# A sum over graph edges: 8 or 4 of 32 destination blocks by row gathers, and with or without a cast in the gather

## The chip, the cores and the metric

The kernel runs on one core of one Trainium2 chip. The metric is the device time of one execution in microseconds (us). TensorE does the matmuls, VectorE the comparisons and elementwise work, ScalarE copies and casts out of PSUM, GpSimd (POOL in the profile) issues the row gathers, and SyncE (SP) issues the plain loads and stores. The engines run on their own and wait for each other by semaphores; each takes its instructions in the order in which the program was written.

## The reference

There are 4096 nodes with 128 float32 features and 65536 edges. Each edge adds the feature row of its source node to the output row of its destination node:

```python
num_nodes, num_edges, dim = 4096, 65536, 128
output = np.zeros((num_nodes, dim), dtype=np.float32)
for i in range(len(edge_index_src)):
    output[edge_index_dst[i]] += node_features[edge_index_src[i]]
```

## The kernel before

The output is made in 32 destination blocks of 128 rows. The feature rows are kept in two parts, a rounded one and the rest, side by side as 256 values (`xr` in SBUF, `x3d` in DRAM, 1 KB a row), so that matmuls in the reduced float32 format add up to the full value; the two halves of a result are added at the end.

**Pass 1** (before the loop) holds the edges as 24 chunks of 22 columns by 128 partitions, worked on in six quads of four chunks. It ranks the edges of each chunk by destination block and moves them with matmuls against permutation matrices, so that in `sa` and `sbk` every chunk has, for every destination block, a column of up to 128 edges, one in each partition: `sbk` holds the source block, `sa` a code of the source and destination rows within their blocks.

**Gathered blocks.** The first `KG` = 8 destination blocks (L27) are summed from gathered rows. For a block `d` and a quad `q`, `gather` (L320 to L327) issues four indirect DMAs on POOL; each fetches 128 rows of `x3d` by the indices in `gidx` into a quarter of a tile `rows`, which is declared float32r, while `x3d` is float32. There are six such tiles (`GB`, pool `xg`). `gather_key` compares the destination rows with a counter on VectorE (`ohg`) and casts the result on ScalarE (`ohgf`, L333). `gather_sum` (L341) does four matmuls of 256 columns into `psg`; after six quads the block is evacuated (L348). The 48 tiles stand in a fixed `order`. `add_up(n)` sums up to the n-th, and before each sum it issues gathers up to `GB` tiles ahead (`issue`, L361), of which the last has to wait until the tile before the current one is summed and its buffer free.

**Dense blocks.** The other 24 blocks are made by matmuls alone. For each block, `pass2` sorts the edges once more by their 32 source blocks. It works on a group of blocks together (`GROUPS`, L28: 4, 4, 8 and 8), in steps: for a group of four, bucket comparisons with column sums (L551, L560), payloads (L495), counts and ranks (L574, L577, L512); for a group of eight, bucket comparisons with sums (L480, L488), payloads, running counts (L503), masking and ranks (L507, L512); then, for each pair of blocks, permutations on VectorE (L212, tile `p`), matmuls (L533), a ScalarE copy `pa` (L536) and the keys of the pair on VectorE (L543). With the keys, `onehots` (L591) builds two one-hot matrices of 128 by 4096 on VectorE (tile `oh`). `blocks(k)` (L601) multiplies them for four source blocks into `psa`, one of two PSUM buffers, giving the counts of each source row in each destination row, and ScalarE casts these into `a` (L603). `product(k)` (L607) multiplies `a` with `xr`, 256 columns at a time, into `pso`.

**The loop** (L662 to L687) has one slot for each dense block, 24 in all. In each slot VectorE first makes what is pending of keys, then the key one-hots (`prepare`), the one-hots of the next slot's block, and the first part of the steps that the table `STEPS` (L30 to L32) names for this slot as (group, number of steps). TensorE does the slot's 32 block matmuls, in four turns with the 32 products of the previous slot's block, then the matmuls of the steps, then `add_up(n)`, where n spreads the tiles that are left evenly over the slots. Group 0 and two steps of group 1 are done before the loop, and nine tiles are summed there. ScalarE's queue holds the casts of the key one-hots ahead of the slot's casts of `a`. Order and steps are written out by hand; there is no planner.

Of the kernel before, what the change touches and what calls it, by code (L numbers as in the profile page):

```python
# [9 lines left out]
F32 = mybir.dt.float32  # L10
# [13 lines left out]
CODE0 = 0x2000  # L24
ROW0 = P + (CODE0 >> 7)
BIG = 4096.0
KG = 8  # L27
GROUPS = (4, 4, 8, 8)  # L28

STEPS = {0: [(1, 1)], 1: [(1, 1)], 2: [(1, 1), (2, 1)], 3: [(2, 1)], 4: [(2, 1)], 5: [(2, 1)],  # L30
         6: [(2, 1)], 7: [(2, 1)], 9: [(2, 1), (3, 1)], 11: [(2, 1)], 12: [(3, 2)], 13: [(3, 1)],
         14: [(3, 1)], 16: [(3, 1)], 18: [(3, 1)], 20: [(3, 1)]}  # L32


WIN = ((0, 7, 0, 64), (7, 14, 4, 100), (14, NJ, 20, P))
# [49 lines left out]
def _fast(ctx, tc, X, src32, dst32, out, ident, fmax, flag_i, x3d, T):  # L85
# [66 lines left out]
    for r in (slice(0, P), slice(P, ROW0)):  # L152
        for i in range(2):
            nc.sync.dma_start(
                out=x3d[r, i * P:(i + 1) * P].rearrange("p (j m) -> p j m", j=4),
                in_=zrow[:r.stop - r.start, i])
# [122 lines left out]
    def place(q):  # L279

        at = (q % 2 * QH + q // 2) * 4
        return slice(at, at + 4)
# [21 lines left out]

    gidx = sb1.tile([P, NCH, KG], I32, name="gidx")
    gkey = sb1.tile([P, NCH, KG, 2], U16, name="gkey")
    gslo = sb1.tile([P, NCH, KG], U16, name="gslo")

    def gather_keys(q):
        cs = place(q)  # L310
        code = sa[:, cs, :KG].bitcast(U16)
        V.tensor_single_scalar(out=gslo[:, cs, :], in_=code, scalar=7, op=OP.logical_shift_right)
        V.tensor_single_scalar(out=gkey[:, cs, :, :], scalar=127, op=OP.bitwise_and,
                               in_=code[:, :, :, None].to_broadcast([P, 4, KG, 2]))
        V.scalar_tensor_tensor(out=gidx[:, cs, :], in0=sbk[:, cs, :KG], scalar=float(P),
                               in1=gslo[:, cs, :], op0=OP.mult, op1=OP.add)
# [3 lines left out]
    def gather(d, q):  # L320
        t = xg.tile([P, 4, 2 * P], F32R, name="rows", tag="xg")
        for l in range(4):
            G.indirect_dma_start(  # L323
                out=t[:, l, :], out_offset=None, in_=x3d[:, :],
                in_offset=bass.IndirectOffsetOnAxis(ap=gidx[:, place(q).start + l, d:d + 1],
                                                    axis=0))
        rows[d, q] = t  # L327
# [33 lines left out]
    def issue(n):  # L361
        nonlocal issued
        while issued < min(n, ready):
            gather(*order[issued])
            issued += 1
# [81 lines left out]
    for t in p2b:  # L447
        for h in range(2):
            S.copy(out=t[:, h * NH:(h + 1) * NH, (1 - h) * 64:(2 - h) * 64],
                   in_=zero.to_broadcast([P, NH, 64]))  # L450
    first = [KG + sum(GROUPS[:g]) for g in range(len(GROUPS))]
    keys2 = {}

    def pass2(g):

        d0, gd = first[g], GROUPS[g]
        kk = 4 if gd % 4 == 0 else 2
# [153 lines left out]
    def flag():  # L611

        ng = len(GROUPS)
        full = sb1.tile([P, NCH * NB], BF16, name="full", tag="o0")
# [11 lines left out]

    todo = [pass2(g) for g in range(len(GROUPS))]

    def run(fs):
        for f in fs:  # L630
            f()
# [27 lines left out]
    n0 = summed  # L659
    flat_slots = [(g, i) for g, gd in enumerate(GROUPS) for i in range(gd)]  # L660
    slots = len(flat_slots)
    for slot, (g, i) in enumerate(flat_slots):  # L662
        n = n0 + (len(order) - n0) * (slot + 1) // slots
        run(pending)
        steps = [todo[pg].pop(0) for pg, k in STEPS.get(slot, ()) for _ in range(k)]
        pending = [f for st in steps for f in st[2:]]
# [115 lines left out]
```

## Time and profile before

| | |
|---|---|
| time, median of 3 runs | 442.68 us (440.57 to 444.94) |
| the profiled execution | 445.17 us, span 443.4 us |
| mean granted TensorE clock | 0.815 of full |
| busy in the span | TensorE 306.0 us, VectorE 263.1, POOL 217.9, ScalarE 191.0 |
| indirect DMAs | 192, 25.18 MB |

The span runs from the first to the last instruction; the execution is a little longer. A busy TensorE is one with a matmul in flight, not one at its peak. The time before the first `psa` matmul, 140.4 us, is pass 1 and the first steps of pass 2; the rest is the loop and the last block's products.

### The profile page before, as it was taken

The page shows a single profiled execution, that of the slowest core. Times are in us where ns is not written, and L with a number is a line of the kernel's source. Part 1 is how long each engine was busy: PE and PEld are TensorE (multiplying, and loading weights), DVE is VectorE, ACT ScalarE, POOL GpSimd, SP SyncE. Part 2 cuts the span into 40 slices and gives each one's busy share as a digit, 9 for nine tenths or more (in the row PEclk, how much of TensorE's full clock was granted, in tenths as well). Part 3 has the DMA queues.
Part 4 walks back from the last instruction along what each step waited for, and adds up shares of the span by engine and source line. Part 5 has one row for each costly group of instructions (what it writes and reads, how often), then busy time and mean ns, then how long its engine had stood idle before and what let it go on. Part 6 is the DMA issues. An engine that isn't in the chain of part 4 may idle for free.

```text
span 443.4 us, 8588 instructions
## 1 busy us (share of the span) xinstructions
PE 306.0 (69%) x3580; PEld 278.1 (63%) x3584; DVE 263.1 (59%) x438; ACT 191.0 (43%) x381; POOL 217.9 (49%) x222
## 2 busy tenths in 40 slices
PE   0887646736606688795966868487888668686896
PEld 0677435725605378694965858487787657575886
DVE  5999825927209516797826548158985428282740
ACT  3764213206103544372454344355355426363572
POOL 6534747156563334574836444636773544545300
PEclk9999658665655578897989759979799889798899
DMA  9833423043341222233333222422432333424200
GB/s 254 239 129 90 103 65 85 14 94 70 69 99 38 59 49 49 65 79 78 86 76 89 66 61 44 106 55 52 108 86 54 79 88 73 89 55 102 61 14 19
DMA packets 42504, 35.37 MB, mean 80 GB/s; under 512 B 5344, under 2 KB 42208, under 8 KB 42464
## 3 DMA queue, kind: packets, MB, share of 16 engines
q0 software_dynamic: 27648, 25.18, 25.9%
q1 hardware_dynamic: 14672, 9.11, 7.2%
q8 instruction: 28, 0.46, 0.4%
q10 hardware_dynamic: 144, 0.52, 0.3%
q14 instruction: 12, 0.10, 0.1%
HBM read 28.31 MB, written 6.49 MB: 78 GB/s over the span
## 4 chain that ended last, share of the span: by engine, by line
PE 45%; DVE 14%; issue 14%; ACT 12%; another core or an unknown queue 12%; DMA 1%; ACTq 0%; DVEq 0%
PE pso L607 18%; PE psa L601 10%; ACT a L603 6%; PE psg L341 5%; DVE oh L212 4%; PE ps L533 4%; DVE v L273 3%; ACT ohgf L333 3%; DVE p L212 3%; PE psm L297 2%; PE psr L512 2%; ACT cum L252 1%; PE psb L488 1%; PE psc L577 1%
## 5 line engine op out<-in xcount | busy, mean ns | idle before, releaser
L323 POOL DMA_INDIRECT rows<-x3d,gidx x192 | 200.8, 1046 | 184.6 <-PE psg L341 110.3
L603 ACT CAST a<-psa 128x512 fp32r<-128x512 f32 x192 | 104.6, 589 | 102.2 <-remote 63.6
L607 PE MATMUL pso<-xr,a 128*128 128x256 f32 x768 | 125.9, 312 | 0.0
L601 PE MATMUL psa<-oh 128*128 128x128 bf16 x768 | 71.7, 235 | 66.9 <-issue 40.8
L607 PEld LDWEIGHTS pso<-xr,a 128*128 128x128 f32 x768 | 108.6, 210 | 0.0
L601 PEld LDWEIGHTS <-oh 128*128 128x128 bf16 x768 | 52.5, 105 | 78.4 <-issue 73.3
L212 DVE TENSOR_TENSOR oh<-psi,slo 128x4096 bf16<-128x4096 uint16 x24 | 54.9, 2286 | 33.6 <-PE psa L601 30.9
L212 DVE TENSOR_TENSOR p<-psi,rank 128x768 bf16<-128x768 uint16 (+4 forms) x120 | 52.9, 509 | 12.4 <-ACT rank L517 8.9
L212 DVE TENSOR_TENSOR oh<-psi,dlo 128x4096 bf16<-128x4096 uint16 x24 | 54.8, 2282 | 0.0
L543 DVE TENSOR_SCALAR slo<-pa 128x128 uint16<-128x128 uint16 x12 | 2.7, 226 | 83.9 <-ACT pa L536 83.9
L341 PE MATMUL psg<-rows,ohgf 128*128 128x256 f32 x192 | 38.4, 354 | 4.5 <-ACT ohgf L333 4.5
L341 PEld LDWEIGHTS psg<-rows,ohgf 128*128 128x128 f32 x192 | 33.8, 256 | 5.1 <-ACT ohgf L333 5.0
L297 PE MATMUL psm<-v,p 128*128 128x64 bf16 x512 | 25.3, 208 | 16.7 <-issue 14.8
L252 ACT ACTIVATE cum<-psc,minus 128x512 bf16<-128x512 f32 (+1 forms) x36 | 21.9, 649 | 29.1 <-remote 12.7
L333 ACT CAST ohgf<-ohg 128x512 fp32r<-128x512 bf16 x48 | 27.9, 624 | 13.5 <-DVE ohg L212 13.5
L297 PEld LDWEIGHTS <-p 128*128 128x128 bf16 x512 | 21.8, 107 | 19.0 <-issue 16.6
L533 PEld LDWEIGHTS <-p 128*128 128x128 bf16 x576 | 19.3, 107 | 16.4 <-DVE p L212 15.6
L212 DVE TENSOR_TENSOR ohg<-psi,gkey 128x512 bf16<-128x512 uint16 x48 | 18.3, 417 | 0.0
L197 POOL TENSOR_TENSOR xr<-xf,xr 128x512 fp32r<-128x512 f32 x8 | 11.8, 1495 | 13.3 <-ACT xr L193 13.3
L249 PEld LDWEIGHTS <-sums 128*128 128x128 bf16 x126 | 11.4, 109 | 9.8 <-issue 6.6
L533 PE MATMUL ps<-v,p 128*128 128x32 bf16 x480 | 17.0, 195 | 0.0
L245 PE MATMUL psc<-oh,early 128*128 128x512 bf16 (+1 forms) x33 | 13.6, 412 | 3.3 <-ACT cum L252 2.7
(83 smaller groups left out, 252.1 us busy)
## 6 DMA issues: line engine op xcount, KB each, us to landing
x3d<-xr SPq DMA_DIRECT2D x4, 1024.0 KB
rows<-x3d,gidx POOLq DMA_INDIRECT x192
xf<-in_node_features_dram SPq DMA_DIRECT2D x4, 512.0 KB
out_dram<-res SPq DMA_DIRECT2D x32, 64.0 KB
raw<-in_edge_index_src_dram ACTq DMA_DIRECT2D x1, 512.0 KB
raw<-in_edge_index_dst_dram SPq DMA_DIRECT2D x1, 512.0 KB
x3d<-p SPq DMA_DIRECT2D x2, 64.0 KB
x3d<-p SPq DMA_DIRECT2D x2, 32.0 KB
```

Source lines behind the costliest of these rows:

```text
L212: V.tensor_tensor(out=dst.rearrange("p i (m k) -> p i m k", k=2), in0=io.rearrange("p i (m k) -> p i m k", k=2), in1=keys2[:, :, None, :]. ...
L245: PE.matmul(out=psc[:, :n * P], lhsT=early[:], rhs=oh1q(q)[:, 4 * j0:4 * (j0 + n), :].rearrange("p t b -> p (t b)"), start=True, stop=j0 + ...
L252: S.activation(out=cum[:, :, 4 * j0:4 * (j0 + n)], func=RELU, bias=minus[:], in_=psc[:, :n * P].rearrange("p (t b) -> p b t", b=NB))
L273: V.tensor_tensor(out=v1[q][:, :, k, :].rearrange("p t (b k) -> p t b k", k=2), in0=oh1q(q).rearrange("p t (b k) -> p t b k", k=2), in1=ke ...
L297: PE.matmul(out=psm[:, l * 64:(l + 1) * 64], lhsT=t[:, l % 2, j, :], rhs=v1[q][:, 4 * j + l].rearrange("p k b -> p (k b)"), start=j == 0, ...
L323: G.indirect_dma_start(out=t[:, l, :], out_offset=None, in_=x3d[:, :], in_offset=bass.IndirectOffsetOnAxis(ap=gidx[:, place(q).start + l, ...
L333: S.copy(out=ohg[d, q][:], in_=oh[:])
L341: PE.matmul(out=psg[d][:, :2 * P], lhsT=oh[:, l, :], rhs=t[:, l, :], start=q == 0 and l == 0, stop=q == NQ - 1 and l == 3)
L533: PE.matmul(out=ps2[:, d % 2 * NB:(d % 2 + 1) * NB], lhsT=p2b[d % 2][:, c, :], rhs=T2["v"][:, c, d // kk, :, d % kk], start=c == 0, stop=c ...
L601: PE.matmul(out=psa[:, i * P:(i + 1) * P], lhsT=oh[0][:, s, :], rhs=oh[1][:, s, :], start=True, stop=True)
L603: S.copy(out=a[:, k * 4:k * 4 + 4, :], in_=psa[:].rearrange("p (s m) -> p s m", s=4))
L607: PE.matmul(out=pso[:, :2 * P], lhsT=a[:, s, :], rhs=xr[s // 16][:, s % 16, :, :].rearrange("p v f -> p (v f)"), start=s == 0, stop=s == N ...
```

## The change

The number of gathered blocks goes from 8 to 4, the dense blocks from 24 to 28, in groups of 4, 4, 4, 8 and 8. The steps table is written anew for five groups and 28 slots. The gather's destination is seen as float32, as its source is, so that no conversion of type stands in the DMA; TensorE still reads the tile as float32r. With this there are 24 gathered tiles (96 indirect DMAs) in place of 48 (192); nine of them are summed before the loop, as before.

```diff
-KG = 8
-GROUPS = (4, 4, 8, 8)
-
-STEPS = {0: [(1, 1)], 1: [(1, 1)], 2: [(1, 1), (2, 1)], 3: [(2, 1)], 4: [(2, 1)], 5: [(2, 1)],
-         6: [(2, 1)], 7: [(2, 1)], 9: [(2, 1), (3, 1)], 11: [(2, 1)], 12: [(3, 2)], 13: [(3, 1)],
-         14: [(3, 1)], 16: [(3, 1)], 18: [(3, 1)], 20: [(3, 1)]}
+KG = 4
+GROUPS = (4, 4, 4, 8, 8)
+
+STEPS = {0: [(1, 1)], 1: [(1, 1)], 2: [(1, 1)], 3: [(2, 1)], 4: [(2, 1)], 5: [(2, 1)],
+         6: [(2, 1), (3, 1)], 7: [(2, 1)], 8: [(3, 2)], 9: [(3, 1)], 10: [(3, 1)], 12: [(3, 1)],
+         13: [(4, 1)], 14: [(3, 1)], 15: [(3, 1)], 16: [(4, 2)], 17: [(4, 1)], 18: [(4, 1)],
+         20: [(4, 1)], 22: [(4, 1)], 24: [(4, 1)]}
...
             G.indirect_dma_start(
-                out=t[:, l, :], out_offset=None, in_=x3d[:, :],
+                out=t[:, l, :].bitcast(F32), out_offset=None, in_=x3d[:, :],
```

## Rows read from the trace of the kernel before

**Rows 1.** Page: busy us, share of the span, instructions of each engine.
```profile
PE 306.0 (69%) x3580; PEld 278.1 (63%) x3584; DVE 263.1 (59%) x438; ACT 191.0 (43%) x381; POOL 217.9 (49%) x222
```
**Rows 2.** Page: the chain that ended last, shares of the span.
```profile
PE 45%; DVE 14%; issue 14%; ACT 12%; another core or an unknown queue 12%; DMA 1%; ACTq 0%; DVEq 0%
```
**Rows 3.** Waits in the loop: who for whom, us, times, longest.
```profile
DVE slo L543 <- ACT pa L536: 67.1, 10, 9.4
ACT a L603 <- remote: 63.6, 23, 5.2
...
ACT a L603 <- PE psa L601: 33.9, 42, 2.8
```
**Rows 4.** Loop by slot: stretch, length, each engine's busy (count), PEclk, DMA, GB/s.
```profile
140.41:158.99 18.58, 13.33 (x96) 10.02 (x95) 10.54 (x12) 9.73 (x18) 6.39 (x7) 0.50 0.26 56
...
187.94:195.48 7.54, 7.12 (x75) 6.76 (x75) 7.54 (x8) 6.29 (x14) 5.23 (x5) 1.00 0.32 72
195.48:210.06 14.58, 9.04 (x74) 8.50 (x74) 11.47 (x17) 5.91 (x12) 8.14 (x9) 0.80 0.37 82
...
302.07:313.07 11.00, 8.70 (x74) 8.10 (x73) 10.79 (x13) 5.72 (x11) 8.86 (x8) 0.87 0.34 74
...
338.39:351.75 13.36, 8.68 (x75) 8.13 (x73) 7.42 (x8) 6.20 (x12) 7.50 (x9) 0.87 0.37 83
...
365.06:374.52 9.46, 7.42 (x74) 6.87 (x72) 7.55 (x9) 6.27 (x13) 3.78 (x5) 1.00 0.31 72
...
420.62:428.15 7.53, 7.33 (x76) 6.84 (x74) 4.88 (x7) 5.74 (x12) 0.00 (x0) 1.00 0.04 12
...
140.41:440.06 299.65, 228.34 (x2346) 212.66 (x2345) 176.47 (x280) 143.63 (x288) 145.17 (x139) 0.85 0.31 69
```
**Rows 5.** Timeline of the slot at 338.39: start, us, engine, instructions [idle before].
```profile
343.32 0.94 POOL L323 DMA_INDIRECT rows<-x3d,gidx  x1 [0.30 <-issue]
...
345.56 0.59 ACT L603 CAST a<-psa 128x512 fp32r<-128x512 f32 x1 [3.54 <-remote]
...
347.69 0.58 ACT L603 CAST a<-psa 128x512 fp32r<-128x512 f32 x1 [1.53 <-PE psa L601]
...
348.67 2.06 PE L607 MATMUL pso<-xr,a 128*128 128x256 f32 x8
349.90 1.07 ACT L603 CAST a<-psa 128x512 fp32r<-128x512 f32 x2 [1.63 <-PE psa L601]
```
**Rows 6.** Timeline of the slot at 420.62.
```profile
424.49 1.20 PE L607 MATMUL pso<-xr,a 128*128 128x256 f32 x8
```
**Rows 7.** The chain in order of time: start, us, what.
```profile
427.16 0.94 PE psg L341 x8
```
**Rows 8.** Groups by line and form: count, busy us, mean ns, idle before.
```profile
L212 DVE TENSOR_TENSOR oh<-psi,slo 128x4096 bf16<-128x4096 uint16 x24 | 54.9, 2286 | 33.6 <-PE psa L601 30.9 <-remote 2.7
...
L212 DVE TENSOR_TENSOR ohg<-psi,gkey 128x512 bf16<-128x512 uint16 x48 | 18.3, 417 | 0.0
...
L507 DVE TENSOR_TENSOR cum<-cum,oh 128x6144 bf16<-128x6144 bf16 x2 | 6.7, 3350 | 0.0
```
**Rows 9.** Timeline of TensorE, the slot at 140.41.
```profile
148.12 0.59 PE L574 MATMUL psc<-oh,early 128*128 128x512 bf16 x1 [2.27 <-issue]
...
155.50 2.72 PE L512 MATMUL psr<-cum,identb 128*128 128x96 bf16 x32 [0.78 <-ACT cum L580]
```
**Rows 10.** Timeline of the slot at 397.57.
```profile
408.95 1.72 PE L533 MATMUL ps<-v,p 128*128 128x32 bf16 x48
```
**Rows 11.** Timeline of the slots at 302.07 and 313.07.
```profile
306.82 3.42 DVE L495 TENSOR_TENSOR v<-oh,sa 128x3072 bf16<-128x3072 bf16 x2
310.15 5.02 DVE L503 TENSOR_TENSOR cum<-cum,oh 128x512 bf16<-128x512 bf16 x11
...
316.95 1.07 PE L601 MATMUL psa<-oh 128*128 128x128 bf16 x8 [2.00 <-ACT ohgf L333]
```
**Rows 12.** The gather's line: duration ns min/median/max, first and last start.
```profile
L323 POOL DMA_INDIRECT rows<-x3d,gidx x192: 934/937/4059, 38.4 to 415.7; - x192
```

## The prediction

> **What bounds the kernel now.** I read the profile in five steps. First the busy shares [rows 1]: no engine is full; TensorE leads with 69%. The chain that ended last [rows 2] gives TensorE 45% and leaves 12% to an unknown queue and 14% to "issue", time that the profile can't put down to anybody. So the question is where TensorE stands still although it is the longest. The waits inside the dense loop [rows 3] say where: ScalarE's cast of `a` waits 63.6 us for a "remote" releaser and 33.9 us more for `psa`, in a loop of 299.65 us (last line of [rows 4]).
>
> The fourth view is the one that decides: the loop cut at the first `psa` matmul of each of its 24 slots [rows 4]. Every slot but the first does the same 32 block matmuls and 32 product matmuls, but slots last from 7.5 to 17 us. The column to look at beside the length is POOL, whose work in the loop is the gathers: seven or eight gathers of 0.94 us each [rows 12] are two gathered tiles, 3.8 us is one, 0.00 none. The slot at 420.62 has no gather, no pass-2 matmul, eight `psg` matmuls, and takes 7.53 us with TensorE busy 7.33. Slots of that content with two tiles take 14.58 us (195.48), 13.36 us (338.39) and 11.00 us (302.07); with one tile 7.54 us (187.94) and 9.46 us (365.06).
>
> The fifth is the timeline of the slot at 338.39 [rows 5]: while the second tile is gathered, the casts of `a` for blocks 4, 5 and 6 start 3.54, 1.53 and 1.63 us late, though their matmuls stand as issued long before, and the eight products behind them take 2.06 us, against 1.20 us in a slot without gathers [rows 6]. So gathering is not TensorE's or ScalarE's work, but it goes with 6 us of standstill where two tiles come in one slot. I don't know the mechanism; the argument needs only that the stall comes with the gathers.
>
> **The change, part by part.** Before the loop (the first 140.41 us) the order of work stays: nine tiles are summed there in both kernels, and the same gathers are issued: 192 less the 138 that start in the loop ([rows 4], last line, which counts one begun before), so 54.
>
> *Stalls that go.* Slots before: 12 with seven or eight gathers, 9 with five or six, 3 with three or none (all 24 stand in the view of [rows 4]). Price of a two-tile slot: 13.36 - 7.53 = 5.8, 14.58 - 7.53 = 7.1, 11.00 - 7.53 = 3.5; I take 6.0, the first being nearest to what most of the loop looks like. Price of a one-tile slot: 7.54 - 7.53 = 0.0 and 9.46 - 7.53 = 1.9; I take 1.0 for the nine. That is 12 x 6.0 + 9 x 1.0 = 81 us. After the change 96 gathers are left, 42 of them in the loop; the sums are spread as 15 tiles over 28 slots, never two in one, so a slot releases one buffer at most and about 11 slots gather one tile. There I take 1.4 (nearer to the later row): 15 us. Gone: 66 us. Lower bound: the 63.6 us of waits [rows 3] less 11 x 1.9, or 43 us; upper: 81 us.
>
> *Sums that go.* 24 tiles of four `psg` matmuls: eight hold the chain for 0.94 us [rows 7], so 0.48 us a tile with its start: -11.5 us. POOL loses 24 x 4 x 0.94 = 90 us of work and VectorE and ScalarE their key one-hots; neither engine sets the end, so nothing more.
>
> *Four dense slots come.* A slot without gathers and sums is 7.53 - 0.95 = 6.58 us: +26.3 us. It hides VectorE's two one-hots, 2 x 2.29 = 4.6 us [rows 8], and ScalarE's eight casts; that cover fails only where VectorE comes late, two terms on.
>
> *One pass-2 group of four comes.* Two pairs of permutations, 1.72 us of matmuls each [rows 10]: 3.4 us. Its counts and ranks: in the slot at 140.41 they ran from 148.12 to 155.50 + 2.72 [rows 9], 10.1 us, at a granted clock of 0.50 ([rows 4]: 1.2 GHz, the lower of the two levels). In a warm loop the matmul part would halve, so between 5 and 10.1; I take the upper end, since the ScalarE steps between don't shrink and the column sums ahead of them come on top. Together +13.5 us.
>
> *VectorE late in two places.* The steps table puts payloads and running counts of a group of eight into one slot (slots 8 and 16). Before, that happened once: 3.42 + 5.02 = 8.4 us on VectorE in a slot of 11 us, and the next slot's key one-hot came late, so that ScalarE's queue and then `psa` waited 2.00 us [rows 11]. Now these slots are about 8 us, and VectorE's list in them is 4.6 + 8.4 + 0.3 = 13.3 us: some 5 us late, twice, +10 us. Between 0 (the next slot absorbs it) and 2 x (8.4 + 3.35), with the masking step of the following slot [rows 8] fully exposed: 24 us. Queued behind are the key one-hot, the next slot's one-hots and, over ScalarE's in-order queue, the casts of `a`.
>
> *The cast.* No row shows a gather without one. A gather costs POOL 0.94 us and the next follows 0.30 us later [rows 5, 12], so it is POOL that sets the pace. I take 0: POOL has no work that the end waits for. If the cast is what stalls TensorE, up to the 15 us left above; a loss would be POOL time only, and POOL has half of the loop free.
>
> **Sum**: -66 - 11.5 + 26.3 + 13.5 + 10 = -27.7 us on the profiled execution of 445.17 us (span 443.4 and 1.8 around it): 417.5. That execution is 2.5 us above the median of three, 442.68; on the median's scale 415.0, so **415 us**. With every term at its good end -81 - 11.5 + 26.3 + 8.4 + 0 = -58, which is also all that the cast could add; at its bad end -43 - 11.5 + 26.3 + 13.5 + 24 = +9.
>
> **Rivals.** (1) *The cast is the cause of the stall.* For: the stall is in no view explained by sizes; TensorE and the gather share only SBUF. Against: nothing shows a difference. Then the remaining 15 us go as well: 400 us or less. (2) *VectorE becomes the bound.* In the loop it is busy 176.5 of 299.65 us ([rows 4], last line), idle 123, of which 67.1 are waits for a pair's permuted keys [rows 3], that come when the slot's TensorE work ends. The change adds 4 x 4.6 us of one-hots and about 9 us of pass 2, and takes 24 x 0.42 us of key one-hots [rows 8]: +17 us. If its idle time stays as it is, the loop grows by 17 us: 460 us, slower. Against: those waits are as long as the slots, and these shrink; the point of decision is a slot without gathers that is longer than 8 us. In a weaker form, with about half of it, the gain is eaten to within 1% of no change. (3) *The stall is not the gathers'.* Then each dense slot costs the mean, 299.65 / 24 = 12.5 us, four cost 50, less 11.5 for the sums: 481 us. Against: the slot at 420.62 has none of it. Here stands the rule of the Trainium skill ("SBUF — State Buffer", "SBUF: two separate sides") that DMA and engine ports can't contend and TensorE never waits for another engine's accesses; by it this rival would be the likely one and the time 481 us, and the trace does not agree: the lengths in [rows 4] follow the gathers. (4) *The change doesn't do what it says*: both the number of gathers and the float32 view are plain in the diff; this could only be that the view still converts, which is my forecast again.
>
> **How the numbers follow.** Forecast (404 to 434): 0.57. Rival 1, below 404: 0.15. Rival 2 in its weak form, 438 to 446: 0.11; between that and the forecast, 434 to 438: 0.04. Rival 2 in full, or rival 3: 0.13. A measurement of this kernel can't tell less than about 1% (438.3 to 447.1 us) from no change. So faster by over 1%: 0.57 + 0.15 + 0.04 = 0.76; within: 0.11; slower: 0.13. The range leaves out half of rival 1 and the slower cases, about 0.2: 395 to 446 us; the forecast's own range is 404 to 434.
>
> **What would show it.** Slots: 28 in the loop, those without gathers at 6.6 to 8.5 us; no slot with 7 us of POOL; ScalarE's "remote" wait for `psa` down from 63.6 us to below 25. Slots 9 and 17 with `psa` waiting on a late key one-hot or one-hot. The gather's 0.94 us unchanged. The prediction is wrong if slots without gathers still show casts of `a` 2 us or more late (rival 3), if VectorE's waits for `pa` stay near 67 us over the loop (rival 2), or if one-tile slots equal those without (rival 1).

## The result and the profile after

In the measurement of the change the kernel after took 416.39 us (median of 4 runs, 413.23 to 419.17) against 442.44 us (440.57 to 444.94): ratio 0.941 (0.932 to 0.949). The prediction said 415. The profiled execution took 413.23 us with a span of 411.5 us; the mean granted clock rose from 0.815 to 0.863. In the experiments, on three chips, the kernel before took 327 to 328 us (medians; of its 75 executions there one took 821.33 us, with no trace kept, and no other over 332.43). On the one chip where the kernel after ran again it was **7% slower** than the kernel before, and on another chip it was about as much slower with the cast put back. Both results have to be explained. (Slots are counted from 0; a bare slot is one with a dense block's own matmuls and nothing else.)

The page after, busy time of each engine, answers to [rows 1]; the chain that ended last answers to [rows 2].

```profile
PE 306.8 (75%) x3920; PEld 277.9 (68%) x3924; DVE 280.4 (68%) x439; ACT 200.3 (49%) x399; POOL 117.6 (29%) x126
...
PE 50%; DVE 22%; ACT 11%; another core or an unknown queue 9%; issue 6%; DMA 1%; DVEq 0%; ACTq 0%
```

POOL fell from 217.9 to 117.6 us, TensorE's work is nearly what it was. On the chain, "issue" and the unknown queue, 14% and 12% before, are 6% and 9%. The waits in the loop (who for whom, us, times, longest), against [rows 3]:

```profile
DVE slo L544 <- ACT pa L537: 49.2, 12, 6.7
ACT a L604 <- PE psa L602: 48.8, 75, 4.2
...
ACT a L604 <- remote: 5.2, 3, 2.5
```

The cast's "remote" wait went from 63.6 to 5.2 us, but its wait for `psa`, 33.9 us before, is 48.8 us now: of the two together, 97.5 us, there are 54.0 left, in a loop with 32 more casts. The loop by slot, columns as in [rows 4]:

```profile
138.11:154.84 16.73, 12.36 (x92) 9.12 (x92) 9.61 (x9) 8.41 (x14) 6.48 (x7) 0.50 0.22 63
...
163.40:172.98 9.58, 7.66 (x114) 7.29 (x113) 6.88 (x10) 4.85 (x9) 3.79 (x4) 1.00 0.22 63
...
181.42:189.52 8.10, 6.17 (x66) 5.80 (x64) 6.57 (x7) 4.76 (x9) 4.50 (x4) 1.00 0.32 86
189.52:202.39 12.87, 11.35 (x130) 9.66 (x128) 8.54 (x7) 9.56 (x19) 0.00 (x0) 1.00 0.02 6
...
230.92:247.19 16.27, 11.21 (x102) 10.74 (x100) 15.93 (x19) 5.86 (x13) 0.00 (x0) 0.79 0.04 10
...
314.11:333.47 19.36, 11.07 (x98) 10.33 (x97) 19.02 (x21) 5.15 (x11) 4.92 (x4) 0.74 0.13 38
...
342.04:347.88 5.84, 5.84 (x66) 5.66 (x64) 5.84 (x8) 4.24 (x8) 0.00 (x0) 1.00 0.01 3
```

Look at the fifth group, POOL: 0.00 is a slot that gathers nothing. A bare slot takes 5.84 us with TensorE busy throughout (342.04); the same TensorE work beside four gathers takes 8.10 us (181.42). Slots 9 (at 230.92) and 17 (at 314.11) are long in another way: VectorE is busy 15.93 of 16.27 and 19.02 of 19.36 us. The loop, from the first `psa` matmul to the last matmul, is 270.0 us instead of 299.65.

### The profile page after: what moved, and what is told of

Its sections match the earlier page's. It is cut to its first block, busy times and chain, and to the rows that moved or that the text cites. A ratio compares the mean times of both kernels' runs of the same rounds, so it can differ in the third digit from the quotient of the medians.

```text
span 411.5 us, 9143 instructions
## 1 busy us (share of the span) xinstructions
PE 306.8 (75%) x3920; PEld 277.9 (68%) x3924; DVE 280.4 (68%) x439; ACT 200.3 (49%) x399; POOL 117.6 (29%) x126
## 4 chain that ended last, share of the span: by engine, by line
PE 50%; DVE 22%; ACT 11%; another core or an unknown queue 9%; issue 6%; DMA 1%; DVEq 0%; ACTq 0%
PE pso L608 17%; PE psa L602 10%; DVE oh L213 9%; ACT a L604 5%; PE ps L534 5%; PE psm L298 4%; PE psr L513 3%; DVE cum L504 2%; DVE v L274 2%; PE psg L342 2%; ACT cum L253 2%; DVE v L496 2%; DVE cum L508 2%; ACT ohgf L334 2%
## 5 line engine op out<-in xcount | busy, mean ns | idle before, releaser
L324 POOL DMA_INDIRECT rows<-x3d,gidx x96 | 100.5, 1046 | 188.6 <-PE psa L602 127.6
L604 ACT CAST a<-psa 128x512 fp32r<-128x512 f32 x224 | 121.2, 590 | 56.5 <-PE psa L602 48.8
L213 DVE TENSOR_TENSOR oh<-psi,slo 128x4096 bf16<-128x4096 uint16 x28 | 64.0, 2284 | 5.4 <-PE psa L602 3.4
L213 DVE TENSOR_TENSOR p<-psi,rank 128x448 bf16<-128x448 uint16 (+1 forms) x128 | 56.7, 508 | 12.9 <-ACT rank L518 12.9
L213 DVE TENSOR_TENSOR oh<-psi,dlo 128x4096 bf16<-128x4096 uint16 x28 | 63.9, 2281 | 0.0
L298 PEld LDWEIGHTS <-p 128*128 128x128 bf16 x512 | 22.3, 110 | 17.9 <-issue 15.5
L342 PE MATMUL psg<-rows,ohgf 128*128 128x256 f32 x96 | 18.9, 338 | 6.3 <-ACT ohgf L334 6.3
L513 PEld LDWEIGHTS <-identb 128*128 128x128 bf16 x160 | 12.8, 114 | 11.8 <-issue 11.2
L342 PEld LDWEIGHTS psg<-rows,ohgf 128*128 128x128 f32 x96 | 15.4, 229 | 6.8 <-ACT ohgf L334 6.7
L513 PE MATMUL psr<-cum,identb 128*128 128x96 bf16 (+1 forms) x128 | 12.3, 271 | 9.9 <-DVE cum L508 8.3
L334 ACT CAST ohgf<-ohg 128x512 fp32r<-128x512 bf16 x24 | 14.4, 624 | 10.6 <-DVE ohg L213 10.6
```

The lines of the kernel that those rows point to most:

```text
L213: V.tensor_tensor(out=dst.rearrange("p i (m k) -> p i m k", k=2), in0=io.rearrange("p i (m k) -> p i m k", k=2), in1=keys2[:, :, None, :]. ...
L298: PE.matmul(out=psm[:, l * 64:(l + 1) * 64], lhsT=t[:, l % 2, j, :], rhs=v1[q][:, 4 * j + l].rearrange("p k b -> p (k b)"), start=j == 0, ...
L324: G.indirect_dma_start(out=t[:, l, :].bitcast(F32), out_offset=None, in_=x3d[:, :], in_offset=bass.IndirectOffsetOnAxis(ap=gidx[:, place(q ...
L334: S.copy(out=ohg[d, q][:], in_=oh[:])
L342: PE.matmul(out=psg[d][:, :2 * P], lhsT=oh[:, l, :], rhs=t[:, l, :], start=q == 0 and l == 0, stop=q == NQ - 1 and l == 3)
L513: PE.matmul(out=psr[:, :NCH * gd], lhsT=identb[:], rhs=T2["c"][:, :, :, s, :].rearrange("p c i k -> p (c i) k"), start=s == 0, stop=s == N ...
```

## The experiments

Twelve runs, each compared with the kernel before on its own chip.

**The change with the cast put back.**

```diff
-                out=t[:, l, :].bitcast(F32), out_offset=None, in_=x3d[:, :],
+                out=t[:, l, :], out_offset=None, in_=x3d[:, :],
```

> The changed kernel with the cast put back into its gathers (the float32 view taken away, nothing else). Theory A, the stall comes with the gathers whatever their type: the time stays within 1% of the changed kernel's 416 us, slots with one gathered tile lose some 2 us on late casts of the counts, as they do without the cast. Theory B, the cast is part of the price: slower than the changed kernel by 5 to 15 us (421 to 431), with more than 3 us lost in a slot with one tile.

351.77 us against 327.95: ratio 1.068 (1.059 to 1.077). The kernel before itself is 114 us faster than in the first measurement, and the changed structure is the slower one.

**The kernel before without the cast**, twice, on two chips.

```diff
-                out=t[:, l, :], out_offset=None, in_=x3d[:, :],
+                out=t[:, l, :].bitcast(F32), out_offset=None, in_=x3d[:, :],
```

> The kernel before with the float32 view alone, still 8 gathered blocks. Theory A (the number of gathers, not their type): 442 us within 1%, and slots in which two tiles are gathered still last 13 to 15 us. Theory B (the cast): those slots fall to 9 or 10 us and the time to 390 to 415.

> The kernel before with the float32 view of the gather's destination alone, once more. If the kernel before runs at 442 us in these rounds: rival 1 (the cast makes the stall) wants 375 us or less, the theory that any gather makes it wants 435 to 445. If the kernel before runs at 328 us: the same again, 327 to 329.

Ratios 0.998 (0.995 to 1.002) and 1.000 (0.996 to 1.005). The cast costs nothing here; the kernel before never ran at 442 us in these rounds, so the first branch of the second expectation could not be tried.

**Plain loads in place of gathers**, from the 15th tile on (the rows that come are not those that the sums ask for).

```diff
         for l in range(4):
+            if issued >= 14:
+                at = ROW0 + (d * 4 + l) * P
+                nc.sync.dma_start(out=t[:, l, :].bitcast(F32), in_=x3d[at:at + P, :])
+                continue
```

> The kernel before, in which the tiles from the fifteenth on are filled by plain loads of 128 rows each from SyncE's queue in place of indirect DMAs from POOL (the same bytes into the same buffers, not the rows that the sums ask for). If it is the data coming into SBUF that holds up TensorE: no change, 435 to 450 us, late casts of the counts over 60 us in the loop. If it is POOL's descriptor work or the row-wise transfer: the late casts fall below 20 us and the time to 370 to 400.

**No gathers and no transfer**, from the 15th tile on: the sums read one tile that is kept.

```diff
-GB = 6
+GB = 5
...
+        if issued >= 14:
+            rows[d, q] = kept[0]
+            return
```

> The kernel before, in which the sums from the fourteenth tile on all read one tile that was gathered once; no gather and no transfer takes their place, the matmuls stay (one gather buffer fewer, and the sums are not those of the reference). If the stall comes with the gathers: no late casts of the counts, slots of 7 to 9 us where VectorE allows, 365 to 390 us. If the stall belongs to the slots or to the sums: 435 us or more.

327.97 and 328.21 us, ratios 0.999 (0.996 to 1.002) and 0.999 (0.996 to 1.003). With 136 gathers out of the way the time is the same: **in these runs gathering costs the kernel before nothing**. The expectations of the first four runs (the cast put back, the kernel before without it, plain loads, no gathers) all started from the first measurement's times, 416 or 442 us, and none of them came true.

**Both kernels again, unchanged**, so that their traces can be laid side by side.

> The kernel before, word for word, so that its own trace can be laid beside those of the experiments. Theory A (the stall beside the gathers belongs to the conditions of the first measurement, not to the kernel alone): about 328 us, loop about 226 us instead of 299.65, no cast of a that starts late without its operands missing, time before the loop 96 us instead of 140. Theory B (the earlier 328 us was an exception of those rounds): 440 us and the late casts of the first trace.

> The kernel after, word for word. Theory A (the gain was only the stall that the gathers bring; where there is no stall the four dense slots, the pass-2 group and VectorE's lateness are paid for nothing): 351 to 352 us, ratio 1.07 to the kernel before, the same as with the cast put back (351.77). Rival (the missing cast is worth something in the changed structure although it is worth nothing in the old one): clearly under 350 us. Theory B (the stall is there in these runs): 0.94 of the kernel before, 413 to 419 us.

328.21 us, and 352.43 us with ratio 1.073 (1.070 to 1.076): theory A. The slots of the kernel before in this trace; the last line is their total:

```profile
144.15:151.00 6.85, 6.85 (x75) 6.68 (x73) 6.54 (x12) 5.27 (x11) 5.11 (x6) 1.00 0.46 105
...
223.73:241.53 17.80, 12.02 (x103) 11.56 (x101) 17.46 (x23) 5.86 (x13) 13.93 (x11) 0.81 0.42 91
...
250.56:258.29 7.73, 7.12 (x74) 6.76 (x72) 7.39 (x8) 6.07 (x12) 5.90 (x7) 1.00 0.41 93
...
304.99:312.50 7.51, 7.32 (x77) 6.83 (x75) 5.14 (x7) 5.73 (x12) 0.00 (x0) 1.00 0.19 43
...
sum 226.85, PE 203.06 PEld 191.13 DVE 175.95 ACT 142.07 POOL 157.07; mean PE 8.46 PEld 7.96 DVE 7.33 ACT 5.92 POOL 6.54
```

Slots 4 and 15, which took 14.58 and 13.36 us in [rows 4], take 6.85 and 7.73; slot 22, which gathers nothing, 7.51 against 7.53. Gathers come more densely than in the first measurement (150 in 226.85 us, against 138 in 299.65), and nothing waits for them. And of the kernel after:

```profile
131.65:137.50 5.85, 5.85 (x66) 5.67 (x64) 5.85 (x7) 4.52 (x9) 4.49 (x4) 1.00 0.27 75
137.50:150.37 12.87, 11.35 (x130) 9.66 (x128) 9.17 (x7) 9.61 (x20) 0.01 (x1) 1.00 0.10 27
...
175.51:193.99 18.48, 11.02 (x102) 10.55 (x100) 18.14 (x21) 5.90 (x14) 0.00 (x0) 0.82 0.05 15
...
253.36:272.73 19.37, 11.08 (x98) 10.33 (x97) 19.03 (x21) 5.06 (x11) 4.92 (x4) 0.75 0.13 38
...
sum 251.52, PE 224.49 PEld 210.06 DVE 193.80 ACT 151.80 POOL 55.41; mean PE 8.02 PEld 7.50 DVE 6.92 ACT 5.42 POOL 1.98
```

The four-gather slot 4 is now 5.85 us, as long as a bare one; the slots that VectorE makes late are no shorter than in the first measurement (slot 9 takes 18.48 us against 16.27, slot 17 19.37 against 19.36).

**More gathers, and more bytes**, to see whether the stall can be brought back. One issues every gather from the 15th tile on twice, the other adds eight plain loads a slot (both have five row buffers in place of six):

```diff
+            if len(rows_seen) >= 14:
+                G.indirect_dma_start(
+                    out=dup[(4 * len(rows_seen) + l) % ND][:], out_offset=None, in_=x3d[:, :],
...
```

```diff
+        for k in range(8):
+            at = ROW0 + (slot * 8 + k) % 32 * P
+            nc.sync.dma_start(out=dup[k % 4][:], in_=x3d[at:at + P, :])
```

> The kernel before, where from the 15th tile on every gather is issued a second time, into a spare tile that nobody reads (five row buffers in place of six make room): POOL works without a pause in the loop, with about 250 gathers in it instead of 150. Theory A (what stalls TensorE is not the number of gathers, it needs the conditions of the first measurement): no cast of a starts late with its operands there (0 us summed, as in the trace of the kernel before at 328 us); the loop grows to the pace of POOL, 34 tiles x 8 x 1.25 us = 340 us from about 55 us on, so 390 to 400 us, and TensorE's idle time is waits for rows. Rival (the gathers stall TensorE once they come densely enough): late casts of 1 us and more again, 20 us or more in sum, in slots whose rows are there.

> The kernel before with eight plain loads of 128 KB on SP's queue in each slot, 24 MB more from the same DRAM tensor into spare tiles that nobody reads (five row buffers in place of six make room): the bytes that go into SBUF in the loop are about doubled. Theory A (bytes into SBUF don't stall TensorE): 328 to 332 us, late casts 0. Rival (the first measurement's stall was contention for memory or SBUF, which doubled traffic brings back): late casts of 20 us or more in sum, 345 us or more.

480.7 us (one run) with 287 gathers in the loop, and 330.17 us (one run) with the loop's traffic raised from 98 to 200 GB/s. Neither has a cast of `a` that waits for a matmul already over. The 480.7 us lies far above the 390 to 400 expected, above all because the first doubled gather starts at 117.4 us and not at 55: by estimate 34 tiles of 10 us from there end at 457. The waits in that loop:

```profile
ACT a L612 <- PE psa L610: 141.2, 78, 12.9
PEld psg L350 <- DMA rows<-x3d,gidx: 134.3, 69, 5.0
```

TensorE waits for the rows, in its own queue, and ScalarE behind it; that is a wait that the profile can name. So neither the number of gathers nor the bytes by themselves make the first measurement's stall.

**VectorE's lateness.** The kernel after with its steps spread, and then its running counts on POOL:

```diff
-STEPS = {0: [(1, 1)], 1: [(1, 1)], 2: [(1, 1)], 3: [(2, 1)], 4: [(2, 1)], 5: [(2, 1)],
-         6: [(2, 1), (3, 1)], 7: [(2, 1)], 8: [(3, 2)], 9: [(3, 1)], 10: [(3, 1)], 12: [(3, 1)],
-         13: [(4, 1)], 14: [(3, 1)], 15: [(3, 1)], 16: [(4, 2)], 17: [(4, 1)], 18: [(4, 1)],
+STEPS = {0: [(1, 1)], 1: [(1, 1)], 2: [(1, 1)], 3: [(2, 2)], 4: [(2, 1)], 5: [(2, 1), (3, 1)],
+         6: [(2, 1)], 7: [(3, 1)], 8: [(3, 1)], 9: [(3, 1)], 10: [(3, 1)], 11: [(4, 1)],
+         12: [(3, 1)], 13: [(3, 1)], 14: [(3, 1)], 15: [(4, 1)], 16: [(4, 1)], 17: [(4, 1)], 18: [(4, 1)],
```

> The kernel after with its steps table written anew: the third group's first steps two slots earlier, so that payloads and running counts of a group of eight never stand in one slot and no slot has more than about 10 us of VectorE. Theory (slots 9, 13 and 17 of 18.5, 14.0 and 19.4 us are VectorE's lateness): they fall to 9 to 13 us, the loop by 10 to 17 us, 335 to 342 us without the stall, 400 to 407 with it. Rival (VectorE is full over the whole loop, 230 of 251 us, so that spreading only moves its lateness): 348 us or more.

The version with the counts on POOL has a steps table of its own, in which payloads and running counts of a group of eight start in the same slot again (slots 7 and 15):

```diff
-                V.tensor_tensor(out=cums[:, :, c], in0=cums[:, :, c - 1], in1=ohs2[:, :, c - 1],
+                G.tensor_tensor(out=cums[:, :, c], in0=cums[:, :, c - 1], in1=ohs2[:, :, c - 1],
```

> The kernel after with the spread steps table, and the running counts of the two groups of eight (22 additions, 9.3 us on VectorE) on POOL, which has nothing to do for two thirds of that loop; payloads and running counts start in the same slot (7 and 15), masking stays in slots 9 and 17. Theory (where there is no stall VectorE sets the end of the middle slots): 4 to 9 us less than the spread version's 347.95, 339 to 344 us, slots 9 and 17 shorter by 3 to 5 us each. Rival (POOL is too slow for it: the waits for its counts take the place of VectorE's work): 348 us or more, masking waits for POOL. Neither expects it below the kernel before, 328 us.

Spread: 347.95 us, ratio 1.061 (1.057 to 1.065), 4.5 us under the kernel after: the rival was nearly right, the lateness moves more than it goes. With the counts on POOL: 342.78 us, 1.046 (1.042 to 1.051), 5.2 us less again, as expected; how much of it is the move to POOL and how much the other table was not separated. The spread version's slots 9 and 17:

```profile
175.78:192.61 16.83, 11.85 (x100) 11.42 (x100) 16.49 (x19) 5.80 (x13) 0.00 (x0) 0.80 0.06 17
...
252.42:267.66 15.24, 10.28 (x98) 9.80 (x97) 15.03 (x16) 5.06 (x11) 4.09 (x4) 0.89 0.17 48
```

and slots 9, 16 and 17 with the counts on POOL:

```profile
176.81:188.16 11.35, 9.41 (x100) 8.96 (x100) 11.35 (x8) 5.47 (x12) 3.78 (x4) 1.00 0.26 71
...
240.60:254.55 13.95, 9.21 (x70) 8.80 (x68) 11.04 (x8) 5.51 (x12) 10.72 (x8) 0.76 0.18 49
254.55:263.74 9.19, 8.66 (x98) 8.41 (x97) 9.19 (x7) 5.06 (x11) 5.95 (x4) 1.00 0.27 70
```

Slots 9 and 17 shrink by 5.5 and 6.1 us; slot 16 grows by 5.0 (8.96 in the spread version), and slot 11 by 1.6. The same in the kernel before, its last group's payloads and running counts in two slots:

```diff
-         6: [(2, 1)], 7: [(2, 1)], 9: [(2, 1), (3, 1)], 11: [(2, 1)], 12: [(3, 2)], 13: [(3, 1)],
+         6: [(2, 1)], 7: [(2, 1)], 8: [(2, 1)], 9: [(3, 1)], 10: [(2, 1)], 11: [(3, 1)], 12: [(3, 1)], 13: [(3, 1)],
```

> The kernel before with the last group's payloads and running counts in two slots (11 and 12) and two pairs of the third group one slot earlier (8 and 10). If a slot that holds both makes VectorE late by about 5 us (the prediction's term): 3 to 6 us less than the kernel before, 322 to 325 us without the stall. Rival (VectorE has no slack around these slots, so the lateness moves): within 1 us of the kernel before.

328.88 us, ratio 1.003 (1.001 to 1.005): the rival. Slot 13 fell from 17.80 to 13.77 us, and slots 8 to 12 took it back. No version tried beats the kernel before at 328 us.

## Why the prediction was right, and what it did not know

The two pairs of traces separate what the prediction had to add up. Loops of both kernels, and what the first measurement has over the later one:

| | before | after | difference |
|---|---|---|---|
| loop, experiments | 226.85 | 251.52 | +24.7: the work |
| loop, first measurement | 299.65 | 270.01 | -29.6 |
| stall in the loop (first less later) | 72.8 | 18.5 | -54.3 |
| time before the loop, first / later | 140.41 / 97.52 | 138.11 / 95.88 | -2.3 / -1.6 |

So -54.3 + 24.7 - 2.3 = -31.9 us, which is the difference of the spans, 443.4 to 411.5. The forecast of -27.7 had the same two parts with -66 and +38.3. That 415 us lies 1.4 us from the measured 416.39 is therefore luck: it took 11.7 us too much off for the stalls and put 13.6 us too much on for the work, it left out the 2.3 us ahead of the loop, and the profiled execution of the kernel after lies 3.2 us below its median.

What is called the stall here is all that the first loop is longer, and part of it is not standstill. TensorE's busy time for the same matmuls is 228.34 us in the first loop before and 203.06 in the later one, at mean granted clocks of 0.85 and 0.96; after it is 230.37 and 224.49, at 0.92 and 0.95. So 25.3 of the 72.8 us and 5.9 of the 18.5 go with the lower clock, and 19.4 of the 54.3 us that the change gained.

*Stalls that go* (-66): right in kind, too large by 12 us. A two-tile slot costs what was taken: slot 15 loses 13.36 - 7.73 = 5.6, slot 4 14.58 - 6.85 = 7.7. By the gathers that start in each slot there are 11 such slots and 10 with five or six gathers, not 12 and 9, which at the prediction's prices is 76 us and not 81. But in slots where VectorE is late anyway the stall is hidden (slot 13 is 14.13 us long in the first trace and 17.80 in the later), and the sum before is 72.8. After, a one-tile slot loses 2.0 to 2.5 us (slot 4: 8.10 - 5.85 = 2.25) in seven slots and 1.2 in one, not 1.4 in eleven; slot 0 loses 5.1 (16.73 - 11.63), and slots 9 and 13, where VectorE is late, give 3.7 back: 18.5, not 15.

What the stall looks like, timeline of slot 4 of the kernel after in the first measurement:

```profile
184.35 0.64 PE L602 MATMUL psa<-oh 128*128 128x128 bf16 x8
...
185.62 1.66 POOL L324 DMA_INDIRECT rows<-x3d,gidx  x1 [0.30 <-issue]
185.83 0.10 PEld L602 LDWEIGHTS <-oh 128*128 128x128 bf16 x1
186.23 0.59 ACT L604 CAST a<-psa 128x512 fp32r<-128x512 f32 x1 [1.67 <-PE psa L602]
...
186.87 0.38 PE L602 MATMUL psa<-oh 128*128 128x128 bf16 x4 [0.87 <-issue]
```

and the same instructions of the same kernel in the experiments:

```profile
134.59 0.62 PE L602 MATMUL psa<-oh 128*128 128x128 bf16 x8
...
135.02 1.07 ACT L604 CAST a<-psa 128x512 fp32r<-128x512 f32 x2 [0.39 <-PE psa L602]
135.84 1.66 POOL L324 DMA_INDIRECT rows<-x3d,gidx  x1 [0.30 <-issue]
136.04 0.45 PEld L602 LDWEIGHTS <-oh 128*128 128x128 bf16 x8
136.05 0.62 PE L602 MATMUL psa<-oh 128*128 128x128 bf16 x8
...
136.48 1.07 ACT L604 CAST a<-psa 128x512 fp32r<-128x512 f32 x2 [0.39 <-PE psa L602]
```

With the same gathers at the same distance, the cast starts 1.88 us after the start of its matmuls in the one and 0.43 us in the other. TensorE's wait in the first, which the profile gives to "issue", ends 0.05 us after that cast (186.23 + 0.59), so it is a wait for one of the two `psa` buffers: the cast is late first, as the prediction read it, and TensorE behind it. In the first loop before, all 40 pauses of TensorE of over 0.2 us ahead of `psa` matmuls end like this, and 38 casts start more than 0.5 us after both the end of their matmuls and the end of ScalarE's own last work (77.4 us together); in the later trace no cast does.

The longest case stands ahead of the loop. Kernel after, first measurement:

```profile
116.44 1.75 PE L534 MATMUL ps<-vc,p 128*128 128x32 bf16 x48
...
129.16 0.95 POOL L324 DMA_INDIRECT rows<-x3d,gidx  x1 [0.30 <-issue]
131.05 0.21 ACT L537 CAST pa<-ps 128x64 bf16<-128x64 f32 x1 [15.69 <-remote]
...
131.29 0.23 DVE L544 TENSOR_SCALAR slo<-pa 128x128 uint16<-128x128 uint16 x1 [14.81 <-ACT pa L537]
```

and in the experiments:

```profile
87.08 1.70 PE L534 MATMUL ps<-vc,p 128*128 128x32 bf16 x48
...
88.82 0.21 ACT L537 CAST pa<-ps 128x64 bf16<-128x64 f32 x1 [2.37 <-PE ps L534]
...
89.06 0.23 DVE L544 TENSOR_SCALAR slo<-pa 128x128 uint16<-128x128 uint16 x1 [1.50 <-ACT pa L537]
```

The cast starts 12.9 us after its matmuls in the one, when a row of twelve gathers is over, and 0.04 us after them in the other, between gathers; in the kernel before it is 14.2 us, 2.6 us past the last gather. From ScalarE to VectorE it takes 0.03 us in both. So what comes late is what TensorE hands over. The ends of matmuls are modelled, and whether a matmul ends late or the word of it arrives late is not shown.

One sign that the prediction took for the stall is another matter: eight products take 2.06 us at 348.67 [rows 5], and 2.06 us as well in slot 9 of the kernel after (at 238.35), which gathers nothing; both stretches have a granted clock of 0.50.

The stall sets in where the gathers set in. The first 40 us and the rest before the loop, kernel after, first measurement:

```profile
0.00:40.00 40.00, 25.49 (x506) 21.00 (x508) 34.74 (x58) 23.83 (x41) 18.37 (x32) 1.00 0.65 190
40.00:138.11 98.11, 50.89 (x734) 42.35 (x734) 51.36 (x101) 23.12 (x51) 54.59 (x53) 0.64 0.25 71
```

and in the experiments:

```profile
0.00:40.00 40.00, 25.80 (x506) 21.25 (x508) 34.71 (x58) 24.24 (x43) 18.31 (x32) 1.00 0.64 190
40.00:95.88 55.88, 41.85 (x733) 36.03 (x733) 51.33 (x101) 22.49 (x49) 43.70 (x41) 0.82 0.35 97
```

The first gather starts at 38.4 us [rows 12]. Up to 40 us both run alike; then the same 734 matmuls take 98.11 us in the one and 55.88 in the other. So the prediction's reading, that the stall comes with the gathers, fits both traces of the first measurement; no later run had a stall to test it on. What it could not see is that gathers are **not enough** for it. What else the first measurement had is open: the doubled gathers and the doubled traffic did not bring it back, and no trace from the three chips of the experiments has it. The result of the first measurement does not name its chip.

*Sums that go, four dense slots, one pass-2 group* (-11.5 + 26.3 + 13.5 = +28.3): TensorE's busy time in the loop rose by 224.49 - 203.06 = 21.4 us. The bare slot is 5.84, not 6.58, so four cost 23.4: the slot at 420.62 [rows 4] from which it was derived holds eight `psg` matmuls, which with the little beside them cost 7.53 - 5.84 = 1.7 us and not 0.95. Slot 5, which holds the added group's counts and ranks, lasts 12.87 us, 7.0 over a bare slot, four `psg` matmuls included; "the upper end", 10.1, was the wrong choice, since that row was taken at a granted clock of 0.50 and slot 5 had 1.00.

*VectorE late in two places* (+10): the places are right, slots 9 and 17, idle on TensorE for 16.27 - 11.21 = 5.1 and 19.36 - 11.07 = 8.3 us. As a difference it is only 24.7 - 21.4 = +3.3 us, because the kernel before has such slots too (slot 13: 17.80 - 12.02 = 5.8; slot 2 alike). [rows 11] show 2.00 us of it there: slots 12 and 13 together take 25.13 us in the first trace and 25.28 in the later, so the stall only hid VectorE's lateness.

*The cast* (0): right. Even in the first measurement the 54 gathers before the loop, with the cast and without, go with 140.41 and 138.11 us, so rival 1 fails there as well, and gathers without a cast still stall their slots by 2.2 us.

*Rival 2*, VectorE as the bound, did not come in the first measurement, where its waits for `pa` fell from 67.1 to 49.2 us. In the experiments its numbers come out: VectorE's work in the loop rises by 193.80 - 175.95 = 17.9 us (the rival said 17), its idle time does not fall (50.9 and 57.7 us), and the loop grows by the sum, 24.7. But TensorE's work rises by 21.4 us of it, and spreading and moving VectorE's work gave only 4.5 and 5.2 us back, so that VectorE alone is the bound is not shown.

*Rival 3* had the sign that the experiments show. Beside it stood the rule of the Trainium skill ("SBUF — State Buffer", "SBUF: two separate sides") that transfers and engine accesses don't contend. In the experiments the traces agree: 25 MB more in the loop came with 330.17 us against 327.24, and with no late cast. In the first measurement there was a stall, and whether the two sides had part in it no run here shows. The price of rival 3, 12.5 us a dense slot, was wrong; (251.52 - 226.85) / 4 = 6.2 us is what one costs, sums and pass 2 included.

## What to carry to other kernels

A standstill that the profile gives to "issue" or "remote" may belong to the occasion and not to the kernel alone: run the kernel before again, on another chip, ahead of any change that is meant to remove it; here the sign of the result hung on it. Where an engine waits for "issue", look at what ended just before it went on; here it was the cast that frees its buffer. When a change removes a stall, ask what the stall was hiding, and price each late engine as a difference between the two kernels. A row taken at the lower clock is no price for work that will run at the higher one.

## What the runs showed of the hardware that was not expected

- One program, one core: 442 us on one occasion and 327 to 328 us in four later comparisons on three chips, with gathers of the same length (median 937 and 938 ns each) and the same plain loads.
- A float32 to float32r gather moves in 1 KB packets, one to float32 in 4 KB packets. The gather queue's packets, MB and share of the span, kernel after with the cast put back, and without:

```profile
q0 software_dynamic: 13824, 12.59, 16.4%
```

```profile
q0 software_dynamic: 4608, 12.59, 13.0%
```

  The packets that carry rows are 12288 of 1024 bytes (mean 71.9 ns) in the one and 3072 of 4096 bytes (233.6 ns) in the other: a fifth less time on this queue, and no less for the kernel (351.77 and 352.43 us).
- POOL's additions slowed VectorE's multiplications. Two payloads beside POOL's running counts:

```profile
231.43 16.33 POOL L504 TENSOR_TENSOR cum<-cum,oh 128x512 bf16<-128x512 bf16 x11
...
239.61 4.68 DVE L496 TENSOR_TENSOR v<-oh,sa 128x3072 bf16<-128x3072 bf16 x2
```

  and without them, in the spread version:

```profile
242.19 3.42 DVE L496 TENSOR_TENSOR v<-oh,sa 128x3072 bf16<-128x3072 bf16 x2
```

  4.68 against 3.42 us, while the one-hots kept their 2.28. It is part of why slot 16 grew.
